# One more place for preparation steps in each pair of attention blocks, and filter sums partly added up halfway through a unit

## The chip, the cores and the metric

The kernel runs on one core of one Trainium2 chip. The metric is the device time of one execution in microseconds (us), as the median of several runs. The engines are named as in the profile: PE (matrix multiply; its weight loads are listed as PEld), DVE (vector), ACT (scalar), POOL (GpSimd) and SP, which here issues nearly all DMA transfers. Each engine takes its instructions strictly in the order in which the program lists them, and waits for another engine only where data or a buffer asks for it.

## The reference

The network has two layers over 2048 latent tokens of width 1024. Layer 0 is a pooling mixer beside grouped-query attention (6 query heads of 128, 2 key heads, 2304 keys). Layer 1 is a Hyena long convolution beside a 2-D Fourier mixer. This case needs the attention and the filters of the convolution, which the kernel computes at the same time:

```python
def one_block(qblk):
    s = jnp.einsum('bqhgd,bkhd->bhgqk', qblk, k, preferred_element_type=jnp.float32) * scale
    p = jax.nn.softmax(s, axis=-1).astype(v.dtype)
    return jnp.einsum('bhgqk,bkhd->bqhgd', p, v)
...
h = (hdn @ w3.astype(f32)).reshape(L, HY_ORDER, 2, HY_WIDTH)
...
h = h * decay[:, None, None, :]
h = h / (jnp.sum(jnp.abs(h), axis=(0, 2), keepdims=True) + EPS)
```

Each filter channel is divided by the sum of its absolute values over all 2048 positions and both directions. The output projections of both layers are multiplied by gates that depend on the conditioning, and the Fourier mixer is followed by a 256x256 matrix `fn_w`.

## The kernel before, in words

The program writes the order of each engine's instructions out by hand. Its stages follow each other: input projection of layer 0; attention; output projection of layer 0 with the projection into layer 1; convolution and Fourier mixing; output projection of layer 1. The change touches only the attention stage.

**Blocks and pairs.** Attention is cut into 96 blocks of 128 queries (6 heads, 8 groups of 256 queries, 2 blocks in each), taken in 48 pairs. `BLOCK` (L44) lists the order of the work in a block, two rows for the even and the odd block of a pair while the filters run, and two more for the pairs after that. In a row, S0 to S4 are the scores of the next block in chunks of 512 keys with their maxima, M the maximum over all chunks, E0 to E4 the exponentials of the next block, Z their sum, T0 to T4 the transposes of this block's probabilities with their split into a high and a low part (names ph, pl), V0 to V4 the products with the values, and D and N the division at the end of a pair. Exponentials and high parts are ACT's, maxima and low parts DVE's.

**Other work inside the blocks.** F stands for one step of the filters (`fill`, L1473, which takes the next step of the first generator in `queue`); f is the same in every eighth pair only. p stands for one step of the weights' preparation (`next(prep, None)`, L1516). In the first two rows a pair has five F and six p.

**The preparation** (`weights`, L1403, used through `prep`) splits weights of later stages into a high and a low part and stores them to HBM. It has 296 steps:

- 23 slabs of the input weights of layer 1, four steps each: load; cast (ACT, `wodd`, L1413); subtract (POOL, L1415); nothing; the store goes out in front of the next slab's load.
- 32 slabs of the output weights, 16 of each layer, six steps each: load (L1433); multiply by the gate (POOL, `wraw`, L1435); nothing; cast; subtract; nothing; then the store.
- Two tables for the Fourier mixer, six steps each: load; three times nothing; four products on PE (`fnp`, L1450) with a copy by ACT (`fnM`, L1452); nothing; store. The products write to the one PSUM bank that the filters use as well.

Raw slabs have two buffers, so a load waits for the subtract of the slab two before it. Loads and stores are on SP's queue, among the loads of the queries and the filters' tables.

**The filters** (`filters`, L1123) run through 12 units (6 channel groups, 2 orders). A unit has 8 groups of two position blocks each. A group takes two fills: one computes the raw filter in PSUM (`hacc`), which DVE multiplies by the decay into `ht`; the next one adds up absolute values over the four slices of `ht` into one slot of `rd` (DVE, L1202) and issues the first Fourier step on PE (`fa`), copied by ACT to `X`. In the last group, after its slot, `rd` is added up over its 8 slots into `rs` (DVE, L1208); one fill later PE sums `rs` over the partitions (`smacc`, L1211 and L1212), DVE makes the scales and `sd` from it (L1217 to L1224), and the fill after that issues the last `fa`. So a unit takes 18 fills. Then POOL does a 16-point FFT over `X` (L155 and L158), handed out by `some` (L1135) at 4.4 us of estimated work for each fill, while the next unit is under way; the spectrum is stored four fills after the last of it has been handed out.

**The end of the filters.** When the filters' generator is at its end, `fill` takes all that is left of the preparation at once, gives the filters' memory free, and from the next fill on the output weights of layer 0 are loaded:

```python
if queue and next(queue[0], fill) is fill:
    queue.pop(0)
    if len(queue) == 1:
        for _ in prep:
            pass
        aside.close()
        ready.append(True)
```

Of the kernel before, what the change touches and what calls it, by code (L numbers as in the profile page):

```python
# [12 lines left out]
F32 = mybir.dt.float32  # L13
F32R = mybir.dt.float32r
AF = mybir.ActivationFunctionType
ALU = mybir.AluOpType
AX = mybir.AxisListType
# [3 lines left out]
P = 128  # L21
D = 1024
# [19 lines left out]
PAIRS = [(n, N2 - n) for n in range(1, 8)] + [(0, 8)]  # L42

BLOCK = [  # L44
# [204 lines left out]
def tile_net(ctx, tc, i, k, out, keep=None):  # L249
    nc = tc.nc  # L250
    v, s, g, pe, sy = nc.vector, nc.scalar, nc.gpsimd, nc.tensor, nc.sync
    keep = {} if keep is None else keep

    def pool(stack, name, bufs=1, space=None, **kw):
        if space is not None:
            kw["space"] = space
        return stack.enter_context(tc.tile_pool(name=name, bufs=bufs, **kw))

    def mv(dst, src, eng=None):

        (eng or sy).dma_start(dst.bitcast(F32) if dst.dtype == F32R else dst, src.bitcast(F32) if src.dtype == F32R else src)
# [238 lines left out]
    with ExitStack() as st, tc.manual_schedule(engines=EVERY):  # L500
        sp = pool(st, "a_sb", 2)
# [54 lines left out]
        with ExitStack() as s2:  # L556
# [154 lines left out]
            b = col1[:, PK1["b0"] : PK1["b0"] + 16]  # L711
# [411 lines left out]
    def filters(st, psum, tag, after):  # L1123

        fc = pool(st, "f_c2", 1, side="right")
        sp = pool(st, "f_u", 1, side="right")  # L1130
        dft = fc.tile([P, N2, 2, P], F32, name="fdft")
        late, ops = [], []
        got, room = {}, [0.0]

        def some():  # L1135

            due[0] += 1
            room[0] = min(room[0] + FFT_US, FFT_US)
            while ops and room[0] > 0:
                us, op = ops.pop(0)  # L1140
                room[0] -= us
                if callable(op):
                    op()
                else:
                    late.append((due[0] + FFT_LATE, op))
            if late and late[0][0] <= due[0]:
                sy.dma_start(*late.pop(0)[1])

        due = [0]

        def fetch(u, grp):
            dec = sp.tile([P, 2, P], F32, tag="dec", name="dec", bufs=2)
            sy.dma_start(dec, k["decay"][u // 2, grp])
            hd = sp.tile([P, 2, P], F32R, tag="hd", name="hd", bufs=2)
            n, m = PAIRS[grp]
            mv(hd, hdd[:, n : m + 1 : m - n, :])
            got[u, grp] = dec, hd

        def fetch_w3(u):

            j, o = u // 2, u % 2
            jl = slice(j * P, j * P + P)
            raw = sp.tile([P, 2, P], F32, tag="w3", name="w3")
            for half in range(2):
                sy.dma_start(raw[half * 64 : half * 64 + 64], i["hy_w3"][0].rearrange("p (x c) -> p x c", x=4)[:, 2 * o : 2 * o + 2, jl])
            skr = sp.tile([1, P], F32, tag="skr", name="skr", bufs=2)
            sy.dma_start(skr, i["hy_skip"][0, o : o + 1, jl])
            got[u] = raw, skr

        def split_w3(u):  # L1170
            raw, skr = got[u]
            w = sp.tile([P, 2, 2, P], F32R, tag="w3s", name="w3s", bufs=2)
            s.copy(w[:, 0], raw)
            v.tensor_sub(w[:, 1], raw, w[:, 0].bitcast(F32))
            got[u] = w, skr

        fetch(0, 0)
        fetch_w3(0)
        yield
        sy.dma_start(dft, k["fdft"])  # L1180
        split_w3(0)
        yield
        for u in range(2 * NCH):
            j, o = u // 2, u % 2
            w3, skr = got.pop(u)
            rd = sp.tile([P, 8, P], F32, tag="rd", name="rd")
            X = sp.tile([P, 2, N2, P], F32, tag="X", name="fX", bufs=FILTER_X)
            for grp, (n, m) in enumerate(PAIRS):
                last = grp == 7
                if (u, grp) != (2 * NCH - 1, 7):  # L1190
                    fetch(u + grp // 7, (grp + 1) % 8)
                dec, hd = got.pop((u, grp))
                ht = sp.tile([P, 2, 2, P], F32, tag="ht", name="ht", bufs=2)
                acc = psum.tile([P, 2, 2, P], F32, tag=tag, name="hacc")
                for q in range(2):
                    for x in range(2):
                        w = w3[:, x, ::-1] if q else w3[:, x]
                        pe.matmul(acc[:, q], hd[:, q, :], w, start=x == 0, stop=x == 1)
                after(1, lambda: v.tensor_mul(ht, acc, dec.unsqueeze(2).to_broadcast([P, 2, 2, P])))
                yield  # L1200
                some()
                v.tensor_reduce(out=rd[:, grp, :], in_=ht.rearrange("p a d b -> p b (a d)"), axis=AX.X, op=ALU.add,  # L1202
                                apply_absolute_value=True)
                if u + 1 < 2 * NCH and grp in (3, 6):
                    (fetch_w3 if grp == 3 else split_w3)(u + 1)
                if last:
                    rs = sp.tile([P, P], F32, tag="rs", name="rs")
                    v.tensor_reduce(out=rs, in_=rd.rearrange("p a b -> p b a"), axis=AX.X, op=ALU.add)  # L1208
                    yield
                    sm = psum.tile([P, 512], F32, tag=tag, name="smacc")  # L1210
                    pe.matmul(sm[:, 0:1], rs, ones[:, 0:1], start=True, stop=True)  # L1211
                    pe.matmul(sm[0:1, P : 2 * P], ones[:, 0:1], rs, start=True, stop=True)  # L1212
                    sd = sp.tile([P, 2, 2, P], F32, tag="ht", name="sd", bufs=2)

                    def scaled():
                        idx = o * NCH + j
                        v.tensor_scalar(out=sc_n[:, idx : idx + 1], in0=sm[:, 0:1], scalar1=EPS, scalar2=None, op0=ALU.add)  # L1217
                        rw = sp.tile([1, P], F32, tag="rw", name="rw")
                        v.scalar_tensor_tensor(out=rw, in0=sm[0:1, P : 2 * P], scalar=EPS, in1=skr, op0=ALU.add, op1=ALU.mult)
                        v.reciprocal(sc_n[:, idx : idx + 1], sc_n[:, idx : idx + 1])  # L1220
                        v.tensor_add(ht[0:1, 0, 0, :], ht[0:1, 0, 0, :], rw)
                        v.memset(ht[0:1, 0, 1, :], 0.0)
                        v.tensor_add(sd[:, 0], ht[:, :, 0], ht[:, :, 1])
                        v.tensor_sub(sd[:, 1], ht[:, :, 0], ht[:, :, 1])  # L1224


                    after(2, scaled)
                    yield
                fa = psum.tile([P, 2, 2, P], F32, tag=tag, name="fa")
                for r in range(2):  # L1230
                    for q, b in enumerate((n, m)):
                        if last:
                            pe.matmul(fa[:, r, q], dft[:, b, r, :], sd[:, r, q], start=True, stop=True)
                        else:
                            pe.matmul(fa[:, r], dft[:, b, r, :], ht[:, q], start=q == 0, stop=q == 1)
                after(3, lambda: s.copy(X[:, :, n : m + 1 : m - n, :], fa))  # L1236
                yield
                if last:
                    T = sp.tile([P, 2, N2, P], F32, tag="T", name="fT")
                    ops += [(0.04 + 2.05 * us, fn) for fn, us in fft16(g, X, T, False, g, True)]  # L1240
                    ops.append((0.0, (specd[j][o], X)))
                some()
        while ops or late:
            some()
            yield
# [17 lines left out]
    with ExitStack() as st:  # L1263
        kp = pool(st, "b_k", 1)
        sp = pool(st, "b_sb", 2)
# [193 lines left out]
        def after(n, fn):  # L1459

            pending.append([n, fn])
# [21 lines left out]

        ready = []
        queue = [filters(aside, psF, "f", after), wout()]
        prep = weights()
        dgs = {}
# [121 lines left out]
    with ExitStack() as st, tc.manual_schedule(engines=EVERY):  # L1609
        sp = pool(st, "c_sb", 2)  # L1610
# [221 lines left out]
    with ExitStack() as st, tc.manual_schedule(engines=EVERY):  # L1832
        bp = pool(st, "e_b", 2)
        sp = pool(st, "e_sb", 2)
# [209 lines left out]
        M = [mp.tile([P, 2, 256], F32, tag="m", name=f"M{x}") for x in range(2)]  # L2044
# [381 lines left out]
```

## Time and profile before

| what | us |
|---|---|
| median of 3 runs | 3170.86 (3167.14 to 3171.73) |
| the profiled execution's own time | 3177.3 |
| its span | 3175.5 |
| PE busy | 2937.0 (92%) |
| DVE busy | 2149.7 (68%) |
| ACT busy | 1323.7 (42%) |
| POOL busy | 1132.7 (36%) |

Durations in the profile come from one execution. A line of a group of instructions names the source line, the engine, the operation, the tile written and the tiles read, the count, and durations in ns; a line in order of time begins with its start and its length in us. In square brackets stands how long the engine was idle before the instruction and what ended that. A line of waits names who waited for whom, the total, the count and the longest wait. In a line of windows each engine has its busy time and count of instructions, and then follow the clock that PE was granted (1.00 is full), the share of time that the DMA engines were busy, and GB/s.

### The profile page before, as it was taken

The numbers are of one execution on the slowest core, as the hardware profiler recorded it, in microseconds if no ns is written. First come the engines' busy times: TensorE is split into PE (matmuls) and PEld (weight loads), VectorE is DVE, ScalarE is ACT, GpSimd is POOL, SyncE is SP. The second block draws the span as 40 slices with busy tenths as digits, with TensorE's granted clock in tenths as the row PEclk, the third lists the DMA queues.
The fourth block names the chain that finished last, engine by engine and source line by source line (L and its number), as shares of the span: only waits on it lengthen the run. The fifth ranks groups of instructions, "written<-read, shape, count | busy, mean of one in ns | idle before, by whom it ended". The sixth has DMA issues, their size and how long they took to land. (4 is left out here: it accounts for less than half of the span.)

```text
span 3175.5 us, 46860 instructions
## 1 busy us (share of the span) xinstructions
PE 2937.0 (92%) x16969; PEld 2520.1 (79%) x16969; DVE 2149.7 (68%) x3981; ACT 1323.7 (42%) x3048; POOL 1132.7 (36%) x1091
## 2 busy tenths in 40 slices
PE   7999999799999999999986999999989999988799
PEld 4898888688888888888875778777878777874587
DVE  4676327477777777777764343377879797978556
ACT  4444445365655555556554232322323222231223
POOL 3122122117877778788871344001010010100110
PEclk9999999899999999999998999999999999989899
DMA  6466335534443343333325577689899989976875
GB/s 219 147 206 206 107 135 172 168 100 129 128 134 115 112 148 105 112 118 112 104 77 214 183 268 252 242 268 292 275 307 277 289 275 302 278 235 184 218 205 175
DMA packets 346707, 602.74 MB, mean 190 GB/s; under 512 B 41894, under 2 KB 216168, under 8 KB 336490
## 3 DMA queue, kind: packets, MB, share of 16 engines
q1 hardware_dynamic: 321178, 516.37, 47.9%
q0 software_dynamic: 25152, 83.10, 11.1%
q8 instruction: 134, 2.20, 0.3%
q14 instruction: 99, 0.81, 0.1%
q10 hardware_dynamic: 144, 0.26, 0.0%
HBM read 376.80 MB, written 187.18 MB: 178 GB/s over the span
## 5 line engine op out<-in xcount | busy, mean ns | idle before, releaser
L312 DVE TENSOR_TENSOR pl<-pt,ph 128x512 fp32r<-128x512 f32 (+1 forms) x480 | 299.0, 633 | 171.8 <-ACT ph L309 165.0
L155 DVE TENSOR_TENSOR gB<-gB 128x256 f32<-128x256 f32 (+3 forms) x442 | 351.6, 845 | 47.6 <-ACT gB L1933 43.8
L1338 ACT ACTIVATE pb<-S,mx 128x512 f32<-128x512 f32 (+1 forms) x480 | 310.1, 657 | 161.2 <-DVE mx L1330 161.1
L315 PE MATMUL dacc<-dh,dw 128*128 128x512 f32 x768 | 311.4, 406 | 45.8 <-DMA dh<-h1T 44.5
L309 ACT CAST ph<-pt 128x512 fp32r<-128x512 f32 (+1 forms) x480 | 257.6, 556 | 220.0 <-PE pt L1349 218.8
L1327 DVE TENSOR_REDUCE mx<-S 128x1 f32<-128x512 f32 (+1 forms) x480 | 279.7, 629 | 54.4 <-PE S L317 40.5
L316 PE MATMUL dacc<-dh,dw 128*128 128x512 f32 x768 | 304.1, 396 | 0.0
L317 PE MATMUL dacc<-dh,dw 128*128 128x512 f32 x768 | 303.7, 395 | 0.0
L312 POOL TENSOR_TENSOR wl<-raw,wh 128x256 fp32r<-128x256 f32 x160 | 136.3, 884 | 374.9 <-ACT wh L309 329.7
L1349 PE MATMUL pt<-ident,pb 128*128 128x128 f32 x1728 | 252.2, 276 | 9.5 <-ACT pb L1338 8.4
L1361 PE MATMUL o<-ph,vh 128*128 128x256 f32 x864 | 232.4, 300 | 0.3
L155 POOL TENSOR_TENSOR fT<-fX 128x1024 f32<-128x1024 f32 (+2 forms) x120 | 191.3, 1623 | 115.9 <-ACT fX L1236 114.6
L1349 PEld LDWEIGHTS pt<-ident,pb 128*128 128x128 f32 x1728 | 201.7, 142 | 31.6 <-ACT pb L1338 16.4
L1362 PE MATMUL o<-ph,vl 128*128 128x256 f32 x864 | 218.4, 284 | 2.6 <-DMA vl<-vl 2.6
L155 POOL TENSOR_TENSOR fX<-fT 128x256 f32<-128x256 f32 (+2 forms) x168 | 219.2, 1329 | 2.5
L315 PE MATMUL S<-kh,qh 128*128 128x512 f32 (+1 forms) x480 | 200.0, 417 | 21.3 <-DVE pl L312 10.5
L315 PEld LDWEIGHTS dacc<-dh,dw 128*128 128x128 f32 x768 | 147.0, 191 | 84.7 <-DMA dh<-h1T 42.1
L315 PE MATMUL acc<-wh,hh 128*128 128x256 f32 x672 | 198.1, 295 | 6.6 <-DVE hh L311 3.4
L317 PE MATMUL acc<-wh,hl 128*128 128x256 f32 x672 | 193.9, 289 | 1.0 <-DVE hl L312 0.9
L316 PE MATMUL acc<-wl,hh 128*128 128x256 f32 x672 | 193.7, 288 | 0.9 <-POOL wl L312 0.8
L316 PE MATMUL S<-kl,qh 128*128 128x512 f32 (+1 forms) x480 | 181.9, 379 | 0.7 <-DMA kl<-kT1l 0.7
L317 PE MATMUL S<-kh,ql 128*128 128x512 f32 (+1 forms) x480 | 181.9, 379 | 0.0
(476 smaller groups left out, 7406.3 us busy)
## 6 DMA issues: line engine op xcount, KB each, us to landing
dh<-h1T SPq DMA_DIRECT2D x172, 512.0 KB
spec<-fX SPq DMA_DIRECT2D x12, 2048.0 KB
dw<-wi SPq DMA_DIRECT2D x48, 512.0 KB
gK<-spec SPq DMA_DIRECT2D x48, 512.0 KB
raw<-in_ev_w_in_dram SPq DMA_DIRECT2D x160, 128.0 KB
u<-dev SPq DMA_DIRECT2D x70, 256.0 KB
cu<-u POOLq DMA_DIRECT2D x17, 1024.0 KB, 8.0
wmb<-in_w_mod_dram SPq DMA_DIRECT2D x16, 1024.0 KB
```

The costliest lines, as they stand in the source:

```text
L155: put(out, lambda: v.tensor_tensor(out=out, in0=in0, in1=in1, op=op))
L309: s.copy(hi, src)
L312: lo_eng.tensor_sub(lo, src, hi.bitcast(F32))
L315: pe.matmul(acc, ah, bh, start=first, stop=False)
L316: pe.matmul(acc, ah, bl, start=False, stop=False)
L317: pe.matmul(acc, al, bh, start=False, stop=last)
L1327: v.tensor_reduce(out=B["mx"][:, c : c + 1], in_=S[:, :n], axis=AX.X, op=ALU.max)
L1338: s.activation(B["pb"][:, c * 512 : c * 512 + n], B["S"][c][:, :n], AF.Exp, bias=B["mx"][:, 5:6], accum_out=B["sm"][:, c : c + 1])
L1349: pe.transpose(pt[:, t, :], B["pb"][:, (4 * c + t) * P : (4 * c + t + 1) * P], ident)
L1361: pe.matmul(gr["o"], vh[:, a, :], ph[:, t, :], start=a == 0, stop=False)
L1362: pe.matmul(gr["o"], vl[:, a, :], ph[:, t, :], start=False, stop=False)
```

## The change

The first row of `BLOCK` has a fourth p, after T4, so a pair has seven places for preparation steps while the filters run.

In the filters, `rd` has 6 slots in place of 8. The groups 0 to 4 write slots 0 to 4. After group 4 these five are added up into slot 5. The groups 5, 6 and 7 then write slots 2, 3 and 4, and the last sum goes over slots 2 to 5, so over four slots in place of eight. There are 12 more instructions on DVE.

```diff
-    "T0 p S0 S1 F S2 S3 S4 M T1 f p F D V3 V4 E1 N E3 T2 E0 T3 p E4 E2 F T4 Z",
+    "T0 p S0 S1 F S2 S3 S4 M T1 f p F D V3 V4 E1 N E3 T2 E0 T3 p E4 E2 F T4 p Z",
     "T0 S0 S1 T1 S2 S3 p S4 M p F V0 E3 E0 T2 V1 E1 p F T3 T4 E2 V2 E4 Z",
...
-            rd = sp.tile([P, 8, P], F32, tag="rd", name="rd")
+            rd = sp.tile([P, 6, P], F32, tag="rd", name="rd")
...
-                v.tensor_reduce(out=rd[:, grp, :], in_=ht.rearrange("p a d b -> p b (a d)"), axis=AX.X, op=ALU.add,
+                v.tensor_reduce(out=rd[:, grp - 3 * (grp > 4), :], in_=ht.rearrange("p a d b -> p b (a d)"), axis=AX.X, op=ALU.add,
                                 apply_absolute_value=True)
...
+                if grp == 4:
+                    v.tensor_reduce(out=rd[:, 5, :], in_=rd[:, :5].rearrange("p a b -> p b a"), axis=AX.X, op=ALU.add)
                 if last:
                     rs = sp.tile([P, P], F32, tag="rs", name="rs")
-                    v.tensor_reduce(out=rs, in_=rd.rearrange("p a b -> p b a"), axis=AX.X, op=ALU.add)
+                    v.tensor_reduce(out=rs, in_=rd[:, 2:].rearrange("p a b -> p b a"), axis=AX.X, op=ALU.add)
```

## The prediction

> **What bounds the kernel now.** I read the busy table first, then the windows of the attention stage, the only stage that the diff touches, then the waits of PE in it, and last the instructions in order of time where PE stands still.
>
> ```profile
> PE 2937.0 (92%) x16969; PEld 2520.1 (79%) x16969; DVE 2149.7 (68%) x3981; ACT 1323.7 (42%) x3048; POOL 1132.7 (36%) x1091
> ```
>
> ```profile
> 700.00:800.00 100.00, 98.85 (x676) 90.42 (x675) 77.50 (x154) 60.39 (x158) 75.02 (x58) 1.00 0.36 116
> 1500.00:1600.00 100.00, 95.98 (x650) 86.13 (x650) 78.53 (x154) 59.08 (x157) 72.91 (x60) 1.00 0.34 110
> 1600.00:1640.00 40.00, 34.45 (x227) 30.01 (x226) 24.04 (x52) 20.55 (x56) 33.56 (x25) 0.96 0.25 90
> 1640.00:1660.00 20.00, 15.35 (x98) 12.99 (x97) 9.94 (x22) 10.53 (x29) 19.47 (x22) 0.95 0.21 67
> 1679.30:1709.30 30.00, 6.81 (x17) 5.03 (x17) 1.89 (x3) 1.82 (x3) 5.04 (x4) 0.60 0.32 105
> ```
>
> The columns are PE, weight load, DVE, ACT, POOL, clock, DMA share, GB/s. PE is the bound of this stage: 96 to 99% busy, DVE at 78%, ACT at 60%. So a hole in PE costs its length, and a little work on another engine costs nothing unless PE waits for it. Two places fall out of this picture: 30 us around 1690, where everything is idle, and 1600 to 1660, where POOL is the full engine (19.47 of 20 us).
>
> The hole in order of time:
>
> ```profile
> 1678.89 0.40 PE L317 MATMUL S<-kh,ql 128*128 128x512 f32 x1
> ...
> 1682.49 1.26 POOL L1435 TENSOR_TENSOR wraw<-wraw,wgb 128x512 f32<-128x512 f32 x1 [4.22 <-DMA wraw<-in_od_w_out_dram]
> ...
> 1690.11 1.26 POOL L1435 TENSOR_TENSOR wraw<-wraw,wgb 128x512 f32<-128x512 f32 x1 [4.37 <-DMA wraw<-in_od_w_out_dram]
> 1691.40 0.62 ACT L1413 CAST wodd<-wraw 128x512 fp32r<-128x512 f32 x1 [7.00 <-POOL wraw L1435]
> ...
> 1698.43 3.75 PE L1450 MATMUL fnp<-wraw 128*128 128x256 f32 x8 [19.15 <-DMA wraw<-cst_dftd_dram]
> ...
> 1706.24 3.38 PE L1450 MATMUL fnp<-wraw,wft 128*128 128x256 f32 x8 [4.05 <-DMA wft<-cst_dftd_dram]
> ...
> 1709.27 0.58 PE L315 MATMUL S<-kh,qh 128*128 128x512 f32 x1
> ```
>
> This is the rest of the weights' preparation, drained at one go when the filters end (the loop over prep in fill): two slabs of od_w_out, each load, multiply, cast, subtract, store one after the other, then the two Fourier tables, while PE holds the next scores behind the table's matmuls. The count of steps agrees: 23 x 4 + 32 x 6 + 2 x 6 = 296 steps; 6 places in each of 45 pairs and one in pair 45 make 271, and step 272 is the load of slab 14.
>
> The other holes of PE in the stretch with filters, and the two longest, which lie in the tail after the last filter group:
>
> ```profile
> PE smacc L1211 <- DVE rs L1208: 13.5, 11, 2.1
> PE S L315 <- DVE pl L312: 8.1, 2, 4.3
> ...
> PE fa L1235 <- DVE ht L1199: 4.7, 4, 1.6
> PE fa L1233 <- DVE sd L1223: 4.4, 3, 1.7
> ```
>
> ```profile
> 1631.53 0.62 ACT L1413 CAST wodd<-wraw 128x512 fp32r<-128x512 f32 x1 [4.66 <-POOL wraw L1435]
> ...
> 1633.41 0.50 PE L315 MATMUL S<-kh,qh 128*128 128x512 f32 x1 [4.34 <-DVE pl L312]
> ```
>
> ```profile
> 1657.91 0.80 PE L315 MATMUL S<-kh,qh 128*128 128x512 f32 x1 [3.80 <-DVE pl L312]
> ```
>
> POOL is late with the multiply, behind the FFT; ACT waits for it in order; PE's scores wait for ACT and DVE.
>
> **Term 1, the drain at the filters' end.** With the seventh place, 42 pairs take 294 steps and pair 42 the last two; the filters still end at the first fill of pair 45, as the fills are as many. So there is nothing to drain. PE gets back 1709.27 - (1678.89 + 0.40) = 29.98 us, less the 16 table matmuls, which now run among the scores. Their price is a row of the same shape at full clock:
>
> ```profile
> 1573.54 1.89 PE L1235 MATMUL fa<-ht,fdft 128*128 128x256 f32 x8
> ```
>
> Two such groups are 3.8 us (their own rows, at clock 0.60, say 7.1). The first falls into pair 41, between the last filter group's sums and their matmul, where PE waits anyway. I take -26.2 us; bounds -22.9 (at 7.1) and -27.4 (if that wait hides 1.2 of it). The copies and loads of the two slabs go to engines with 40% to spare.
>
> **Term 2, the tail.** Without preparation after pair 42 both stalls there go. PE's waits alone are 4.34 + 3.80 = 8.1. Block by block, by the maxima of the scores:
>
> ```profile
> L1330 DVE TENSOR_REDUCE mx<-mx x3: 157/158/159, 1604.4 to 1624.0; 128x1 f32<-128x5 f32 x3
> ```
>
> ```profile
> L1330 DVE TENSOR_REDUCE mx<-mx x7: 157/157/159, 1604.4 to 1673.5; 128x1 f32<-128x5 f32 x7
> ```
>
> Two blocks without a stall took 19.6 us, 9.8 each; all six took 69.1, so 69.1 - 58.8 = 10.3 is the most. I take -9.5. The FFT on POOL, freed of 2.6 us a pair, has to keep up with faster blocks; its store is due four fills later, which covers it.
>
> **Term 3, the filters' last sum.**
>
> ```profile
> L1202 DVE TENSOR_REDUCE rd<-ht x96: 1034/1072/1105, 621.6 to 1593.4; 128x128 f32<-128x512 f32 x96
> L1208 DVE TENSOR_REDUCE rs<-rd x12: 1894/1905/2029, 693.0 to 1594.5; 128x128 f32<-128x1024 f32 x12
> ```
>
> ```profile
> 694.94 0.38 PE L1211 MATMUL smacc<-ones,rs 128*128 128x1 f32 x2 [2.10 <-DVE rs L1208]
> ```
>
> The sum over 8 slots takes 1.905 us; over 4 slots it has the shape of the rd rows, 1.072. The matmul that waits for it comes 0.83 us sooner. The mean wait is 13.5 / 11 = 1.23, so the most is 11 x 0.83 = 9.2; some waits are under 0.83, I count 7.8. The waits for sd come through the same DVE queue: 3 x 0.83 = 2.5. And a long wait costs clock afterwards:
>
> ```profile
> 694.00:700.00 6.00, 5.06 (x28) 4.64 (x29) 3.98 (x12) 3.29 (x10) 1.27 (x1) 0.72 0.42 131
> 856.00:862.00 6.00, 4.82 (x34) 4.31 (x35) 4.54 (x14) 3.49 (x10) 0.00 (x0) 1.00 0.95 360
> 1018.00:1024.00 6.00, 4.70 (x27) 4.25 (x27) 3.91 (x10) 3.52 (x10) 1.27 (x1) 0.72 0.37 119
> ```
>
> These are the three 2.1 us waits; two are followed by a clock of 0.72, 6 x 0.28 = 1.7 us each. At 1.3 us the wait should not do that: -3.4. Together -13.7; as shortening one wait may uncover another behind it, I take four fifths, -11; bounds -5 and -15.
>
> The Trainium skill ("TensorE: Matmul & The Clock Gate", Part 1) has the clock halved only after an idle window of about 3.4 us, and by that rule no 2.1 us wait costs clock, term 3 is 3 us smaller and the time is 3131. The two 0.72 windows speak against it.
>
> **Term 4, the sum halfway.** One reduction over 5 slots, 12 times. From 4 slots at 1.072 and 8 at 1.905 a slot costs 0.208, so 5 cost 1.28 us. No reader on PE waits for it: that group's fa matmuls read ht, which is finished earlier. What queues behind it on DVE are the scores' maxima and the next ht. DVE has 22% idle in that stretch, and the nearest row, the last sum of 1.9 us, shows on PE only at its direct readers. I take +1; bounds 0 and 12 x 1.28 = 15.4.
>
> **Term 5, the steps move through the pair.** With six places a slab of six steps had each step always at the same place (load after T3, multiply after S3, cast after E1). With seven, each falls one place earlier from slab to slab. In question is the cast, which stands in ACT's queue ahead of exps and of the casts of ph, with POOL's multiply two places before it.
>
> ```profile
> POOL wodd L1415 <- ACT wodd L1413: 196.3, 18, 66.8
> ACT pb L1338 <- DVE mx L1330: 157.3, 46, 4.4
> ...
> ACT wodd L1413 <- POOL wraw L1435: 9.3, 3, 4.7
> ```
>
> Mostly POOL waits for ACT, not the other way round: outside the tail ACT waited once. The pair's length is twice that of a block, 285.5 / 25 = 11.4:
>
> ```profile
> L1330 DVE TENSOR_REDUCE mx<-mx x26: 157/158/159, 704.6 to 990.1; 128x1 f32<-128x5 f32 x26
> ```
>
> The worst place is the one after M. Between the cast of the slab before, at the place after E1 one pair earlier, and this slab's multiply POOL has four of the five fills' FFT work, 4 x 4.4 us by the kernel's own ration, plus 2.6 for its own two operations, about 20 us. The time for it is the pair less the way from M to E1, which I put at 5 us (an estimate, under half a block): about 18 us. But there ACT stands idle for the maxima (157.3 / 46 = 3.4 us each time), which hides most. SP's store and load move along; SP already waits there for POOL's subtract, so the load goes out when that ends. With the place before it that is two slabs in seven, some nine casts of the 32 slabs of output weights. I take +2.5; bounds 0 and two full stalls of 6.0 (4.34, and a clock of 0.66 over the 5 us after it):
>
> ```profile
> 1633.00:1638.00 5.00, 4.59 (x17) 3.81 (x18) 4.32 (x10) 1.51 (x5) 4.80 (x8) 0.66 0.00 0
> ```
>
> **Sum.** -26.2 - 9.5 - 11 + 1 + 2.5 = -43.2 us. The profiled execution took 3177.3 us beside its span of 3175.5, so 3134.1; it is 6.4 above the median 3170.86, and on the median's scale the forecast is 3128. The stages after attention start earlier and are otherwise the same.
>
> **Rivals.**
>
> *The sums give back what they win.* DVE pays 1.28 + 1.072 - 1.905 = 0.45 us more for each unit, and the piece halfway lands on a maximum or an ht that PE needs; in its favour, the four waits fa <- ht of 4.7 us exist already. At its upper bound term 4 is +15.4: 3128 + 14 = 3142. Against it: 12 single events on an engine that is 78% busy. The Trainium skill ("VectorE: DVE Perf Modes", Rules for kernel authors) speaks for this rival, as it wants few DVE operations and calls tensor_reduce the slowest.
>
> *Casts stall on the way.* Four stalls of 6.0 us more: 3152. Slower than before if the mechanism is general: the multiply late behind the FFT at every cast near M. It decides from 43.2 / 6.0 = 7.2 stalls more; with all nine, 9 x 6.0 = 54, 3182. Against it is ACT's idle time there, and 196.3 us of POOL waiting.
>
> *A new wait for the output weights.* They are loaded after the filters' end and needed when attention ends, 57 us later in both kernels. If the 30 us came back there: 3171 - 9.5 - 11 + 3.5 = 3154. Against it: 8 MB at the 360 GB/s that a window above shows take 23 us.
>
> *The drain stays.* If the filters' end came before the last step, only term 3 were left: about 3163. The count leaves 3 pairs.
>
> **Chances.** Forecast 0.72 (own range 3114 to 3140), sums 0.10, stalls on the way 0.10, as the general mechanism 0.02, output weights 0.03, drain stays 0.03. The first five but the general one are faster by over 0.2% (6.3 us, about what a measurement can tell from no change), the drain just so or not: faster 0.95, same 0.03, slower 0.02. The range goes from all terms at their best, 3171 - 27.4 - 10.3 - 15 = 3118, with 4 us for the spread of the runs, to the sums' and half of the stalls' case: 3114 to 3148.
>
> **What would show it.** The 30 us window of idle is gone and the fnp matmuls stand near 1580 and 1605, 8 in about 2 us. No cast of wodd is later than that. In the tail blocks of 9.8 us. The last sums take 1.07 us and the sums of waits for rs fall from 13.5 to about 5. I am wrong if PE waits of 3 us or more appear with a cast of wodd behind them, or if fa or S matmuls wait for DVE right after the middle sums.

## The result, and the profile after

The changed kernel takes 3151.8 us in the median against 3171.3, a ratio of 0.9931 with a 95% interval of 0.9912 to 0.9950. The forecast was 3128 with a range of 3114 to 3148, so the sign was right, and the gain of 19.5 us is less than half of the 43.2 forecast. The profiled execution took 3148.5 us, its span is 3146.7.

The two places that the change aimed at look as forecast. The windows of the tail, in the columns of the prediction's windows, for the changed kernel:

```profile
1600.00:1640.00 40.00, 37.94 (x257) 33.73 (x255) 28.55 (x61) 23.07 (x61) 20.05 (x11) 1.00 0.33 115
1640.00:1660.00 20.00, 19.14 (x136) 17.16 (x135) 14.31 (x31) 11.70 (x32) 19.30 (x21) 1.00 0.09 27
```

PE is 95 to 96% busy there in place of 77 to 86%. The table matmuls and the three sums, by tile, in the changed kernel:

```profile
L1452 PE MATMUL fnp<-wraw x8: 379/379/382, 1606.9 to 1608.4; 128*128 128x256 f32 x8
...
L1452 PE MATMUL fnp<-wraw,wft x8: 379/379/382, 1625.9 to 1627.5; 128*128 128x256 f32 x8
```

```profile
L1202 DVE TENSOR_REDUCE rd<-ht x96: 1019/1075/1100, 615.3 to 1608.7; 128x128 f32<-128x512 f32 x96
L1207 DVE TENSOR_REDUCE rd<-rd x12: 1305/1319/1350, 658.3 to 1585.1; 128x128 f32<-128x640 f32 x12
L1210 DVE TENSOR_REDUCE rs<-rd x12: 1028/1055/1105, 687.8 to 1609.8; 128x128 f32<-128x512 f32 x12
```

But the waits of PE in the attention stage are other ones. The view of waits of the changed kernel:

```profile
PE S L315 <- DVE pl L312: 10.6, 7, 4.4
PE hacc L1198 <- DMA hd<-hdd: 9.5, 2, 4.8
PE S L315 <- DMA kh<-kT1h: 9.2, 1, 9.2
...
PE smacc L1213 <- DVE rs L1210: 5.5, 6, 1.6
...
PE fa L1235 <- DVE sd L1225: 3.0, 3, 1.3
```

The waits for rs fell from 13.5 to 5.5 and those for sd from 4.4 to 3.0. The wait for the second half's keys is 9.2 us (2.3 before), and 4.85 us for a filter table are new (the other of the two waits for hd stood before as well). The waits of scores for DVE have moved away from the tail.

The view in which everything can be set against everything is the row of the blocks' maxima: its first and last start, here from the first block to block 83 (the last one with filter groups), before and after the change:

```profile
L1330 DVE TENSOR_REDUCE mx<-mx x84: 157/158/159, 614.5 to 1592.7; 128x1 f32<-128x5 f32 x84
```

```profile
L1332 DVE TENSOR_REDUCE mx<-mx x84: 157/158/159, 608.9 to 1608.0; 128x1 f32<-128x5 f32 x84
```

The same 83 blocks take 978.2 us before and 999.1 after. From the starts of single maxima the whole attention stage, from the first maxima to the first matmul of the next stage, divides as follows (us):

| kernel | blocks 0-83 | 83-86 | 86-90 | 90-91 | 91 to the end | whole |
|---|---|---|---|---|---|---|
| before | 978.2 | 31.3 | 49.5 | 38.6 | 54.2 | 1151.7 |
| changed | 999.1 | 34.3 | 37.7 | 8.7 | 52.5 | 1132.3 |

The drain (90-91) and the tail (86-90) give 41.7 us, of which the table matmuls (83-86) take 2.9 back, and the stretch in which nothing was forecast to be lost loses 20.9.

### The profile page after: what moved, and what is told of

Same layout as the page of the kernel before. It is cut to its first block, busy times and chain, and to the rows that moved or that the text cites. A ratio compares the mean times of both kernels' runs of the same rounds, so it can differ in the third digit from the quotient of the medians.

```text
span 3146.7 us, 46856 instructions
## 1 busy us (share of the span) xinstructions
PE 2926.3 (93%) x16969; PEld 2512.2 (80%) x16969; DVE 2155.3 (68%) x3993; ACT 1325.0 (42%) x3048; POOL 1130.4 (36%) x1091
## 3 DMA queue, kind: packets, MB, share of 16 engines
q1 hardware_dynamic: 321178, 516.37, 48.4%
## 5 line engine op out<-in xcount | busy, mean ns | idle before, releaser
L155 DVE TENSOR_TENSOR gB<-gB 128x256 f32<-128x256 f32 (+3 forms) x442 | 351.4, 844 | 50.6 <-ACT gB L1935 46.8
L1329 DVE TENSOR_REDUCE mx<-S 128x1 f32<-128x512 f32 (+1 forms) x480 | 279.4, 627 | 34.8 <-PE S L317 20.6
L315 PE MATMUL S<-kh,qh 128*128 128x512 f32 (+1 forms) x480 | 200.0, 417 | 30.2 <-DVE pl L312 12.9
L155 POOL TENSOR_TENSOR fX<-fT 128x256 f32<-128x256 f32 (+2 forms) x168 | 219.2, 1327 | 2.3
L315 PEld LDWEIGHTS dacc<-dh,dw 128*128 128x128 f32 x768 | 147.3, 192 | 87.8 <-DMA dh<-h1T 43.2
L155 POOL TENSOR_TENSOR fT<-fX 128x1024 f32<-128x1024 f32 (+2 forms) x120 | 190.9, 1619 | 69.8 <-ACT fX L1238 68.4
```

Source lines behind the costliest of these rows:

```text
L155: put(out, lambda: v.tensor_tensor(out=out, in0=in0, in1=in1, op=op))
L315: pe.matmul(acc, ah, bh, start=first, stop=False)
L1329: v.tensor_reduce(out=B["mx"][:, c : c + 1], in_=S[:, :n], axis=AX.X, op=ALU.max)
```

## The experiments

**The parts alone.** First the seventh place without the new sums:

```diff
-    "... E4 E2 F T4 Z",
+    "... E4 E2 F T4 p Z",
```

> The seventh place alone, with the sums as before. Theory A (the queue of SP: a split slab's store waits there for POOL's subtract, and the next load, the filters' tables and the second half's keys stand behind it) has the new PE waits in this kernel as in the changed one: at the keys about 9 us, at one hacc for its table about 5 us, and at scores behind a cast that waits for its raw slab about 4 us; the sums then are worth what the blocks around them show, about 6 us, so 3171 - 20 + 6, about 3158. Theory C (the sum halfway is what costs, by delaying DVE's maxima) has 3130 to 3140 here, with those waits gone.

Measured: 3158.3 us against 3169.4, ratio 0.9968 (0.9954 to 0.9982). Blocks 0 to 83 take 1005.9 us. The waits of PE in it:

```profile
PE S L315 <- DMA kh<-kT1h: 9.7, 1, 9.7
...
PE S L315 <- DVE pl L312: 5.5, 3, 3.9
PE hacc L1198 <- DMA hd<-hdd: 4.7, 1, 4.7
```

So the new waits belong to the place, not to the sums, and theory C falls. Set against the changed kernel, the sums are worth 1005.9 - 999.1 = 6.8 us in these blocks, near the 6 of theory A.

Then the new sums with six places:

```diff
-    "... E4 E2 F T4 p Z",
+    "... E4 E2 F T4 Z",
```

> The sums alone, with six places. Theory A: slightly faster than before, about 3165, the waits for rs near 5 us in total, and the drain of 30 us still there. The prediction's term 3 and 4 had 10 us, so 3161. Theory C: slower than before, 3175 to 3185.

Measured: 3163.3 us, ratio 0.9979 (0.9962 to 0.9996). Blocks 0 to 83:

```profile
L1332 DVE TENSOR_REDUCE mx<-mx x84: 157/158/159, 607.8 to 1576.0; 128x1 f32<-128x5 f32 x84
```

968.2 us, 10.0 less than before. The waits for rs are 5.4 us in all, as expected. 2.2 of the 10.0 us lie in blocks 46 to 52, but not in the wait for the second half's keys: the block in which they are loaded takes 16.6 us in both kernels. Of the whole stage 8.5 us are won. Set against the changed kernel, the seventh place costs 999.1 - 968.2 = 30.9 us in these blocks.

**The sum halfway.** The sums alone, without the sum after group 4; the last sum takes four slots. The groups 0, 2, 3 and 4 are left out of the sums of absolute values.

```diff
-                if grp == 4:
-                    v.tensor_reduce(out=rd[:, 5, :], in_=rd[:, :5].rearrange("p a b -> p b a"), axis=AX.X, op=ALU.add)
...
-                    v.tensor_reduce(out=rs, in_=rd[:, 2:].rearrange("p a b -> p b a"), axis=AX.X, op=ALU.add)
+                    v.tensor_reduce(out=rs, in_=rd[:, 1:5].rearrange("p a b -> p b a"), axis=AX.X, op=ALU.add)
```

> Six places, the last sum over four slots, and no sum halfway: the groups 0, 2, 3 and 4 are left out of the filters' sums of absolute values. Set against the sums alone this prices the sum halfway. The prediction's term 4 has 1 us, so the attention stage 1142 beside 1143.2; if the sum halfway gives back what the shorter last sum wins (first rival), 1131 to 1135.

Measured: 3162.6 us, ratio 0.9980 (0.9966 to 0.9994), the stage 1143.8 us against 1143.2. Up to block 46, where the keys come in, it takes 533.0 us against 533.7. The differences are under 1 us, less than two executions of one kernel differ by (999.1 and 996.5 us in blocks 0 to 83 of the changed kernel, below). So the twelve sums of 1.32 us on DVE have no cost that shows, and the 15.4 us of the first rival are out.

**Where the seventh place loses.** The three largest holes in the order of time, in the changed kernel. A cast that waits for its raw slab:

```profile
756.75 1.28 POOL L1417 TENSOR_TENSOR wodd<-wraw,wodd 128x512 fp32r<-128x512 f32 x1
...
758.06 0.32 SPq L261 DMA_DIRECT2D wi<-wodd  x1
758.43 1.30 SPq L497 DMA_DIRECT2D wraw<-in_od_w_in_dram  x2
...
764.09 0.62 ACT L1415 CAST wodd<-wraw 128x512 fp32r<-128x512 f32 x1 [5.00 <-DMA wraw<-in_od_w_in_dram]
...
766.99 0.80 PE L315 MATMUL S<-kh,qh 128*128 128x512 f32 x1 [4.44 <-DVE pl L312]
```

The keys of the second half:

```profile
1174.64 1.27 POOL L155 TENSOR_TENSOR fX<-fT 128x512 f32<-128x512 f32 x1
...
1175.87 1.45 POOL L1417 TENSOR_TENSOR wodd<-wraw,wodd 128x512 fp32r<-128x512 f32 x1
...
1177.34 0.54 SPq L261 DMA_DIRECT2D we<-wodd  x1
1177.93 0.60 SPq L1435 DMA_DIRECT2D wraw<-in_ev_w_out_dram  x1
1178.62 0.77 SPq L261 DMA_DIRECT2D kh<-kT1h  x1
...
1183.89 0.77 PE L315 MATMUL S<-kh,qh 128*128 128x512 f32 x1 [9.24 <-DMA kh<-kT1h]
```

A filter table:

```profile
1431.15 1.29 POOL L1417 TENSOR_TENSOR wodd<-wraw,wodd 128x512 fp32r<-128x512 f32 x1
...
1432.46 0.57 SPq L261 DMA_DIRECT2D wo<-wodd  x1
...
1435.16 0.58 SPq L261 DMA_DIRECT2D hd<-hdd  x1
...
1440.05 0.77 PE L1198 MATMUL hacc<-w3s,hd 128*128 128x256 f32 x2 [4.85 <-DMA hd<-hdd]
```

All three begin alike: POOL's subtract, late behind FFT work (L155), then SP's store of that slab at once, and then, in SP's order, what somebody needs. SP had waited for the subtract for 8.3, 15.0 and 10.7 us. Its waits for POOL's subtracts in blocks 0 to 83, before and after the change:

```profile
SPq L261 <- POOL wodd L1415: 186.2, 39, 11.6
```

```profile
SPq L261 <- POOL wodd L1417: 234.7, 51, 15.0
```

To see whether these are one execution's chance, the changed kernel ran again:

> The changed kernel once more beside the others: 0.992 to 0.995 of before, with a PE wait of about 9 us for the keys, about 5 us for hd and about 4 us at the scores behind a cast that waits for its raw slab, if these waits belong to the order of the instructions and not to one execution. If they are chance, they are not at the same blocks again.

Measured: ratio 0.9926 (0.9901 to 0.9952), with waits of 9.9 us for the keys, 4.9 for hd and 4.4 at the scores in the same blocks, and blocks 0 to 83 in 996.5 us. They belong to the order of the instructions.

**The store leaves SP's queue.** POOL stores each split slab right behind its own subtract.

```diff
                 g.tensor_sub(w[:, 1], raw, w[:, 0].bitcast(F32))
+                mv(dst, w, g)
                 yield
                 yield
-                mv(dst, w)
```

> The changed kernel with the split slab's store issued by POOL right behind its own subtract, so SP's queue never waits for POOL there. Theory A: the waits of PE for the keys go back to about 3 us, those for hd in the middle of the stage vanish, and casts no longer wait for raw slabs for 4 to 6 us; 15 to 19 us less than the changed kernel, about 3135. Theory B (POOL is overloaded by the denser preparation, its multiply and subtract are late whoever stores): no gain or a loss, 3150 to 3160, as each issue takes POOL some 0.8 us more.

Measured: 3143.8 us, ratio 0.9919 (0.9897 to 0.9941); the stage takes 1121.9 us, 10.4 less than in the changed kernel's first execution and 8.1 less than in its second; the intervals of the ratios overlap. The wait for the keys is 0.6 us and the one for hd in the middle is gone, as theory A has it. Blocks 46 to 52 and 68 and 69 are 18.4 us shorter than in the changed kernel, as much as theory A had in all, and the other blocks up to 83 are 7.8 longer. Casts still wait in this kernel:

```profile
ACT wodd L1415 <- POOL wraw L1437: 21.1, 6, 7.8
ACT wodd L1415 <- DMA wi<-wodd: 15.9, 3, 8.2
```

The casts' waits for POOL's multiply have grown (21.1 us against 10.6), so theory B holds a part; each issue takes POOL 0.6 to 0.7 us. The other line is the one buffer of the split slab, which is free only when its store has landed. The Trainium skill ("Trainium Kernel Development and Optimization", Key Constraints) says that issuing transfers from several engines only saves the sequencer's issue time. Here it also took away what stood behind the wait: 9.2 us of PE for the keys became 0.6.

**The load ahead of the store.** The next raw slab is loaded first, and the store of the slab before comes at the same place behind it:

```diff
-                mv(dst, w)
+                held.append((dst, w))
...
                         sy.dma_start(raw, src[kk * P : (kk + 1) * P, hl])
+                        store_held()
                         yield
```

(The same line follows the load of the input weights; `store_held` issues what `held` has.)

> The changed kernel, with the store of the split slab directly behind the next slab's load, at the same place, for both kinds of slabs. Theory A1 (the raw slab comes late because its load stands behind the store, and keys and filter tables come late because they stand behind it too): the waits of casts for raw slabs go, those of PE for the keys (9 us) and for hd (5 us) stay, 7 to 10 us less than the changed kernel. Theory A2 (what the earlier kernel with the load first won came from its store one place later for the output weights): no gain, within 3 us of the changed kernel, with keys and hd as late as there.

(The earlier kernel is the next one here, which ran first.) Measured: 3135.2 us, ratio 0.9891 (0.9866 to 0.9916). Blocks 0 to 83 take 981.2 us, 17.9 less than changed, so A2 falls. Only the first slab's cast still waits for its raw slab (6.0 us, as before the change). The four casts that did so in the changed kernel now wait for the store of the slab before, 12.5 us in place of 18.2, and the scores behind the one shown above for 1.5 us in place of 4.4. 6.2 us for the keys and 1.8 for hd are left, so A1 was right on what stays and wrong on its size.

With the store of the output weights one place later still, at the place of the multiply (the input weights as above):

```diff
                         sy.dma_start(raw, src[kk * P : (kk + 1) * P, hl])
                         yield
+                        store_held()
                         g.tensor_mul(raw, raw, gb)
```

> The changed kernel with the next slab's load issued before the store of the slab before it; for the output weights the store comes one place later, for the input weights directly behind the load. Theory A: only what hangs on the load comes back, the casts that wait for raw slabs of the input weights (about 7 us of PE); tables and keys still stand behind the store, so about 3144. Theory B: no change from the changed kernel, 3150 to 3154.

Measured: 3130.3 us, ratio 0.9881 (0.9853 to 0.9910); the stage takes 1111.0 us, blocks 0 to 83 977.7. The waits for the keys and for hd in the middle are gone altogether, which neither theory has. The reason stands in SP's order, not in an earlier subtract: one place later the store stands behind the keys (the first of them leaves SP at 1166.3 us, the store at 1175.7) and behind the next filter table. In front of the store that held hd SP still waits 8.6 us for POOL (10.7 in the changed kernel), but PE doesn't wait for what stands behind it. Blocks 46 to 52 are 6.2 us shorter than with the swap alone. Blocks 12 to 26, where both kernels issue the input weights in the same order, differ by 3.5 us the other way, so a few us between single executions say little. What is left on ACT:

```profile
ACT wodd L1421 <- DMA wi<-wodd: 12.9, 4, 5.3
ACT wodd L1421 <- POOL wraw L1445: 6.6, 3, 5.7
```

**Two halves.** The high half is ready after ACT's cast and needs nothing from POOL. It gets a tile and a store of its own, two places after the cast; the low half is stored late as in the kernel before.

```diff
-                w = wp.tile([P, 2, 512], F32R, tag="w", name="wodd")
-                s.copy(w[:, 0], raw)
+                wh = wp.tile([P, 512], F32R, tag="wh", name="wodh")
+                wl = wp.tile([P, 512], F32R, tag="wl", name="wodl")
+                s.copy(wh, raw)
                 yield
-                g.tensor_sub(w[:, 1], raw, w[:, 0].bitcast(F32))
+                g.tensor_sub(wl, raw, wh.bitcast(F32))
                 yield
+                mv(dst[:, 0], wh)
                 yield
-                mv(dst, w)
+                held.append((dst[:, 1], wl))
```

> The load first and the late store, and the split slab in two tiles of its own: the high half is stored from the cast alone, without POOL, the low half later. If the casts that are left waiting in the kernel with the load first (12.9 us for the store of the slab before) hang on the one buffer that both halves share, their waits fall to about 3 us and the time is 3 to 6 us below that kernel's 3130 beside a before of 3169, a ratio near 0.986. If they hang on the raw load, the ratio stays at 0.988; if the 55 more transfers crowd SP's queue, it rises to 0.990 or more.

Measured: 3122.7 us, ratio 0.9855 (0.9828 to 0.9881), the fastest of all kernels here. The blocks, and what SP still waits for:

```profile
L1332 DVE TENSOR_REDUCE mx<-mx x84: 157/158/159, 610.5 to 1580.4; 128x1 f32<-128x5 f32 x84
```

```profile
SPq L261 <- ACT wodh L1422: 94.1, 35, 8.9
SPq L261 <- POOL wodl L1424: 80.6, 26, 8.0
```

The casts' waits for the store of the slab before are gone (12.9 us in the kernel before, 2.3 for the subtract in their place), so they hung on the one buffer, as expected. Of the 7.9 us that blocks 0 to 83 are shorter than in the kernel before, some 3 are not the split's: two holes of 1.6 us that both kernels have are followed by a clock of 0.72 there and of 1.00 here. 969.9 us are left of 999.1, within 2 us of the sums with six places. SP's waits for POOL's subtract fell from 234.7 us in the changed kernel to 184.7 with the swap, 117.6 with the late store and 80.6 here. The stage is 48.4 us shorter than before the change.

**The same with six places.** With the drain again:

> The kernel with the two halves, with six places in a pair in place of seven; the drain at the filters' end comes back. If SP's wait for POOL costs only because the seventh place moves each slab's store from pair to pair into spots where keys or filter tables stand right behind it, the attention stage up to the tail is no more than 3 us shorter than with the sums alone (968.2 us from the first maxima to those of block 83), since with six places the store stood where nothing urgent followed. If the wait cost time all along, it is 10 us or more shorter. In the whole stage about 1141, with the drain.

Measured in a single execution: 3147.4 us beside 3172.9. Blocks 0 to 83 take 963.6 us, 4.6 less than with the sums alone, 4.2 of them in the blocks where the second half's keys are loaded. So it lies between the two expectations, much nearer to the first: before the change SP's waits for POOL (186.2 us in 39) cost PE little, and the keys were the one place where they did. The stage takes 1133.8 us, not 1141; besides the 4.6 us, the drain (90-91) is 34.8 us in place of 40.2 with the sums alone. With the split store the seventh place costs 969.9 - 963.6 = 6.3 us in blocks 0 to 83 and wins 30.5 us of the stage.

## Why the prediction was wrong, point by point

| term | forecast | measured | how |
|---|---|---|---|
| 1, the drain | -26.2 | -27.0 | 90-91: -29.9; the tables' matmuls in 83-86: +2.9 |
| 2, the tail | -9.5 | -11.8 | 86-90: 37.7 against 49.5 |
| 3 and 4, the sums | -10 | -10.0 with six places, -6.8 with seven | sums alone against before; changed against the place alone; blocks 0-83 |
| 5, the steps move | +2.5 | +30.9 (28.3 in the second execution) | changed against sums alone, blocks 0-83 |
| behind block 91 | 0 | -1.7 | 52.5 against 54.2 |

Terms 1, 2 and 4 held, in mechanism and size, and term 3 nearly so. The table matmuls took 8 in 1.9 us, at 1607 and 1626. In term 2 I had bounded the gain by the two undisturbed blocks of 9.8 us; freed of preparation the tail runs at 37.7 / 4 = 9.4. The last sum took 1.055 us (1.072 forecast), the sum halfway 1.32 (1.28), and no cost of it shows (I took 1 us). In term 3 the waits for rs and sd fell by 8.0 and 1.4 us (7.8 and 2.5 forecast). Its 3.4 us of clock came with six places, where the three long waits fell to 1.23 us and the clock behind them is 1.00. In the changed kernel two of them fell only to 1.6 us, with a clock of 0.72 behind them in the profiled execution. In the count of steps the load of slab 14 is step 273, not 272, which changes nothing.

**The step that failed is term 5**, in its sentence on SP: the store and load move along, SP already waits there for POOL's subtract, "so the load goes out when that ends". That is what happened, and I asked only when the load lands for the multiply. I did not list what else is queued behind SP's wait, and priced the step at 2.5 us where it cost 30.9. With six places the store of an output slab always stands after T3 of the even block, and what follows in SP's order did no harm but once: the second half's keys stood behind it before the change too, and their block took 16.6 us, against 12.6 with six places and the split store. With seven it moves through the pair, and in some pairs it stands just ahead of a fill's tables that are needed at once or, with a longer wait, of the keys, while the subtract is still behind the FFT on POOL. I also counted only the 32 slabs of output weights. The 23 slabs of input weights, whose cast stands one place behind the load, move too, and the largest piece of the loss is theirs. I looked for the loss on ACT behind the multiply, took a row that said POOL mostly waits for ACT as a sign of slack, and overlooked that SP waits for the same POOL for about as long. The row itself says less than I read: 124.6 of its 196.3 us, five of its 18 waits, fall before 696 us, when POOL's FFT has not begun (its first row stands at 702.8). By stretches the 30.9 us are 11.6 in blocks 12 to 33 (9.0 in the second execution; casts of input weights that wait for raw slabs; 7.5 of the 11.6 in blocks 12 and 13, behind the cast shown above), 7.4 in blocks 46 to 52 (keys), 6.8 in blocks 68 and 69 (hd), and 5.1 in small pieces. A large hole is followed by a slower clock, so it costs more than its wait; here the windows behind the casts' and the keys' holes in the changed kernel:

```profile
766.00:772.00 6.00, 5.01 (x14) 4.15 (x15) 4.76 (x10) 1.88 (x6) 0.06 (x1) 0.50 0.42 131
...
1183.90:1189.90 6.00, 6.00 (x19) 4.47 (x20) 2.74 (x5) 0.59 (x1) 0.00 (x0) 0.60 1.05 379
```

The runs in which SP is freed step by step take back 17.9, 21.4 and 29.2 us of it with the places and the steps of preparation unchanged: the place itself was sound.

On the rivals: the second, casts that stall on the way, gave 3152, which is the time measured, with 0.10. That the number fits is luck: casts did wait for POOL's multiply (10.6 us of ACT in four waits), but PE's large holes came through SP. The sums did not give back their gain, the output weights made no wait, the drain went. The bound of 12 us for term 5, two stalls, had no row behind it that counted how often a late subtract meets an urgent load, and with it the range ended 4 us short.

What the stages behind attention add isn't settled. They are the same program in all these kernels, and in single profiles the time from the end of attention to the end of the span differs by several us either way: 1409 us before (3175.5 less 1766.25, the first oacc), 1406 in the changed kernel (3146.7 less 1741.18), 1411 in its second execution, 1415 with the two halves. The start of attention moves likewise with no change ahead of it: the first maxima stand at 614.5 us before and at 608.9 in the changed kernel.

## What to carry to other kernels

When a step of a periodic side job gets one more place, its instructions no longer fall at the same spot of each round, and every queue that they wait in has to be read at every spot that they will reach, above all the queue that issues the transfers: list what stands behind a store that waits for a busy engine. A load that is free to go should be issued ahead of such a store, and the store put behind the loads that somebody needs soon, or split so that the part which is ready early doesn't wait for the late one. A total of waits on an engine that isn't the bound (186 us on SP before) says nothing of its harm; what comes next in that queue does.

## What the runs showed of the hardware that I had not expected

A hole of 1.6 us in PE can be enough for a slower clock. Windows of the changed kernel, the first two after waits of 1.61 and 1.57 us for rs, the third after one of 1.25:

```profile
688.00:694.00 6.00, 5.11 (x28) 4.83 (x29) 4.25 (x13) 3.77 (x12) 0.00 (x0) 0.72 0.08 24
860.00:866.00 6.00, 5.43 (x30) 4.98 (x30) 3.92 (x13) 4.19 (x12) 1.28 (x1) 0.72 0.83 268
1022.70:1028.70 6.00, 5.14 (x37) 4.65 (x38) 4.62 (x14) 4.54 (x13) 1.49 (x2) 1.00 0.71 279
```

In the kernel with the sums alone the same waits are 1.23 us, and the clock behind them is 1.00. But the length alone doesn't decide: in the second execution of the changed kernel the holes at the first two places are 1.60 and 1.58 us, and the clock over the 6 us behind them is 1.00. Before the change, one of three holes of 2.1 us had no slower clock either. What decides is not shown. The Trainium skill ("TensorE: Matmul & The Clock Gate", Part 1) asks for an idle window of about 3.4 us; these rows, with 0.72 after less than half of that, do not agree.
